# The sums made ahead get three buffers, a distance of ten weight tiles between load and use, and a place behind the newest low part on VectorE

## The chip, the cores and the metric

The kernel runs on one core of a Trainium2 chip. The metric is the device time of one execution in microseconds; the median of three runs of the kernel before is 1559.39 us (1559.27 to 1561.91).

## The reference

One decoder layer over 256 tokens of width 4096. One input projection feeds three token mixers and their gates; the branches are normalised, gated, joined and sent through one output projection.

```python
h = rmsnorm(x, ln_g)
proj = h @ w_in                                  # 4096 -> 12288
p_x, p_gate, q, k, v, a_gate, s_u, s_gate = jnp.split(proj, _SPLIT_OFFSETS, axis=-1)
y_pool = pool_mixer(p_x, w_pool, pool_scale)
y_attn = stick_breaking_attention(q, k, v)       # 16 heads of 128
y_ssm = s5_mixer(s_u, lam_re, ..., w_glu, b_glu) # diagonal state space, then h @ w_glu (1024 -> 2048)
y = concat(rmsnorm(y_*, g_*) * silu(gate_*))
return rmsnorm(x + y @ w_out) * final_g          # w_out 4096 -> 4096
```

## The kernel before

All large products are in float32, each made of three TensorE products of parts: the high part of the weights times the high part of the rows, low times high, and high times low. Weights come in **tiles** `w` of 128x1024 floats (512 KB): 384 for the input projection and 16 for the GLU, up to tile 400 (`OUT_FROM`), then 128 tiles for the output projection. For each tile ScalarE rounds the tile to its high part (`hi`, `hi_lo`, recorded at line 117) and VectorE subtracts it from the tile to give the low part (`lo`, line 105). TensorE then runs 12 matmuls of 128x512 on the tile (lines 308 to 310): `hi`, `lo`, `hi` for two row slots and two halves of the tokens. A tile has four buffers (`LOAD_AHEAD`), its parts have four (`RING`).

Beside the tiles run side chains: the state space scan (`ssm`, up to about tile 260: VectorE and ScalarE work, with small products `ps_bu` and `ps_y` on TensorE), attention (`ps_z`, `ps_av`), transposes (`ps_c`, `ps_t`), and gates. A tile scheduler puts VectorE, ScalarE and TensorE instructions into one fixed order for each engine, so an instruction whose data are late holds everything behind it on its engine. SyncE's DMA queue (SP) is in the order of the code; a DMA that has to wait for a buffer holds every later one.

The output projection uses a seven-product scheme for pairs of its 2x2 blocks, for which differences of four weight blocks are needed. For 34 of these blocks (`READY`, the words with "r" in `PLAN`) the differences are **made ahead**, by jobs of `sums_ahead` (line 179), one after another between tile 130 and tile 380. Each job loads two weight tiles of the output projection into `pre` (line 183, 2 x 512 KB), makes four subtractions of 128x512 in place on VectorE (shown as line 105), and stores the result to device memory as `sums` (line 197, 2 x 512 KB), from where the output stage loads it as `t`. The job is a generator with ten steps, pumped at 1.36 steps a tile: the two loads in steps one and two, the subtractions three to four steps later, the stores in two steps after those. `pre` has **one** buffer, so a job's first load waits for the stores of the job before. The loop over tiles issues, for tile i, first the load of tile i + 4 and the split of tile i + 2, then the products of tile i, then the side chains and the job's steps.

Of the kernel before, what the change touches and what calls it, by code (L numbers as in the profile page):

```python
# [12 lines left out]
F32 = mybir.dt.float32  # L13
# [4 lines left out]
ALU = mybir.AluOpType  # L18
PSUM = bass.MemoryType.PSUM

P = 128
# [3 lines left out]
NU = 512  # L25
# [20 lines left out]
READY = [(n, int(w[:-1])) for n, line in enumerate(PLAN) for w in line.split() if w[-1] == "r"]  # L46
ALL_SEVENS = sorted(set(sum(SEVENS, [])))
BACK = ((0, 768), (768, 768), (1536, 512))
READY_FROM = 130
READY_BY = 380  # L50
GATE_AT = (-1, 0, 6, 7)
WIDE = 2 * NU
WARM = 8
# [18 lines left out]
OUT_FROM = 24 * 16 + 4 * 4  # L72
# [3 lines left out]
def body(tc, a, out, ctx):  # L76
    nc = tc.nc
    V, S, T, G = nc.vector, nc.scalar, nc.tensor, nc.gpsimd
# [11 lines left out]
    def pool(name, bufs=1, **kw):  # L90
        return ctx.enter_context(tc.tile_pool(name=name, bufs=bufs, **kw))
# [5 lines left out]
    dp = pool("kept", space=bass.MemoryType.DRAM)  # L97
# [6 lines left out]
    def tt(o, x, y, op):  # L104
        V.tensor_tensor(o, x, y, op)  # L105
# [10 lines left out]
    def act(o, x, f, **kw):  # L116
        return S.activation(o, x, f, **kw)  # L117
# [34 lines left out]
    wtiles, htiles, ttiles, sums_kept = {}, {}, {}, {}  # L152
# [23 lines left out]
                nc.sync.dma_start(t[j], sums_kept[units[ui][1], s][:, j])  # L176
            ttiles[i] = t

    def sums_ahead(pl, job):
        b = pl.tile([P, 2, 2, NU], F32, tag="pre", bufs=1, name="pre")  # L180
        i = OUT_FROM + 32 * job[0] + 2 * ORDER[job[0]].index(job[1])
        for j in range(2):
            nc.sync.dma_start(b[:, j], a["ws"][i + j])
            yield
        yield
        yield
        x, y = b[:, 0], b[:, 1]
        tt(x[:, 0], y[:, 0], x[:, 0], ALU.subtract)
        tt(y[:, 0], y[:, 1], y[:, 0], ALU.subtract)
        yield  # L190
        tt(y[:, 1], y[:, 1], x[:, 0], ALU.subtract)
        tt(x[:, 1], x[:, 1], y[:, 1], ALU.subtract)
        yield
        yield
        kept_in = dp.tile([P, 2, 2, NU], F32, name="sums%d_%d" % job)
        for j in (1, 0):
            nc.sync.dma_start(kept_in[:, j], b[:, j])
            yield
        sums_kept[job] = kept_in
        yield  # L200

    def hi_lo(dst_hi, dst_lo, src):
        made = act(dst_hi, src, AF.Copy)
        tt(dst_lo, src, dst_hi.bitcast(F32), ALU.subtract)
        return made

    entries = [0]
# [105 lines left out]
    state = {"s7_out": {}, "out": False}  # L313
# [13 lines left out]
    def square_x(piece):  # L327
        xr = bp.tile([P, 2, NU], F32, tag="k4", bufs=K4, name="xsq")
        nc.sync.dma_start(xr, a["xr"][piece])
        square_sums(x_sums, xr, piece)  # L330

    def norm_x():
        s = cp.tile([P, 2], F32, name="s_x", tag="s_b", bufs=2)
        V.tensor_reduce(s, x_sums, mybir.AxisListType.X, ALU.add)
        rsqrt_mean(rtok, s, 2, D, cp, "rs")
# [409 lines left out]
    def scaled(ps, name):  # L745
        z = bp.tile([P, 2, NU], F32, tag="k4", bufs=K4, name=name)
        times_r(z, ps)
        return z
# [10 lines left out]
    def take_u(z, n):  # L759
        def gen():  # L760
            yield from channels(z, u_parts[n])
            u_done[0] = 4 * n + 4
        side_q.append(gen())
# [3 lines left out]
    def pump(q, n):  # L767
        while q and n > 0:
            try:
                if next(q[0], "end") == "end":  # L770
                    q.popleft()
                    continue
            except StopIteration:
                q.popleft()
                continue
            n -= 1
# [24 lines left out]
    rp = pre_ctx.enter_context(tc.tile_pool(name="ahead", bufs=1, side="right"))  # L801
# [8 lines left out]
    def constants():  # L810
        nc.sync.dma_start(ident, a["cst"][0])
        for i, dst in ((1, tneg), (2, oneneg), (3, maskb)):
            raw = mp.tile([P, P], F32, name="raw", tag="rb", bufs=1)
            nc.sync.dma_start(raw, a["cst"][i])
            act(dst, raw, AF.Copy)
        V.tensor_copy(identb, ident)
# [7 lines left out]
    def start_late():  # L824
        nonlocal lp
        drain(ssm_q)
        ssm_ctx.close()
        lp = late_ctx.enter_context(tc.tile_pool(name="late", bufs=1, side="right", reuse_waits="tile"))
# [10 lines left out]
    def start_out(n):  # L839
        if n == 0:  # L840
            start_end()
        c = [bank(n % 2 * 2 + t, "pm") for t in range(2)]
        o = ep.tile([P, 2, WIDE], F32, tag="o", bufs=2, name="o")
        for h in range(2):
            nc.sync.dma_start(o[:, :, h * NU:h * NU + NU], a["xr"][2 * n + h])
        return c, o
# [102 lines left out]
            hi_lo(hhl[:, 4 * n:4 * n + 4, 0, :], hhl[:, 4 * n:4 * n + 4, 1, :], u_parts[n])  # L949
        return hhl  # L950

    jobs = deque(READY)
    ready_q, ready_steps = deque(), [0]
    ready_q.extend(sums_ahead(rp, job) for job in jobs)
    ready_total = len(READY) * 10
    loaded = split_to = 0
    hhl = None
    delayed = []
    for i, (ui, at, h, s) in enumerate(subs):
        kind, c, nk = units[ui]  # L960
        if ui == 1 and s == 0:
            constants()
        if ui == 1 and s in SQUARE_AT:
            square_x(SQUARE_AT.index(s))
        if ui == 1 and s == 12:
            with tc.high_priority():
                norm_x()
                take_u(scaled(state.pop("ps0"), "suz"), 0)
        if at == 0 and h == 0:
            if ui == LATE_AT:  # L970
                start_late()
            if kind == "out":
                ps, state["o_n"] = start_out(c)
            else:
                ps = [pm.tile([P, NU], F32, tag="c%d" % t, bufs=2, name="pm") for t in range(2)]
            if kind == "glu" and hhl is None:
                hhl = split_glu()
        while loaded < min(len(subs), i + 1 + LOAD_AHEAD + (1 if state["out"] else 0)):
            if loaded == 0:
                load_first()  # L980
            else:
                if loaded < KT // 2:
                    load_x(loaded)
                load(loaded)
            loaded += 1
        while split_to < min(len(subs), i + 1 + SPLIT_AHEAD):
            split(split_to)
            split_to += 1
        if kind == "ag" and c == A_G + 1536 and s >= 2 and s % 2 == 0:
            take_back(s // 2 - 1)  # L990
        rows = hhl if kind == "glu" else xhl
        if seven(i):
            if h == 0:
                if s == SEVENS[c][0]:
                    drain(side_q)
                    pp = products(c)
                mm_seven(i, s, ps, pp, s == SEVENS[c][0], s == SEVENS[c][-1])
                j = SEVENS[c].index(s)
                if c == 3 and j < 2 * len(BACK):
                    lo, wide = BACK[j % len(BACK)]  # L1000
                    b = state["out_rows"].tile([P, 768], F32, tag="y7_%d" % s, name="back")
                    G.dma_start(b[:, 0:wide], state["done"][:, j // len(BACK), lo:lo + wide])
                    parts[j // len(BACK), lo] = b
                if s == SEVENS[c][-1]:
                    state["fg"] = load_fg(c)
                    state["joined"] = join_seven(pp, state["o_n"])
        else:
            pair = htiles.pop(i)
            late = i >= N_SUB - HELD
            into = [ps[t][h] for t in range(2)] if kind == "out" else ps  # L1010
            mm_tok(into, rows, (2 * s, 2 * s + 1), pair, at == 0, at == nk // 2 - 1, (0,) if late else (0, 1))
            if late:
                delayed.append((s, h, pair))
        if at == nk // 2 - 1 and h == (1 if kind == "out" else 0):
            n = nth.get(kind, 0)
            nth[kind] = n + 1
            if (kind, n) != ("out", 3):
                finish(kind, c, n, ps)
        if kind == "out" and c == 0 and h == 1 and s - 2 in ALL_SEVENS and s - 2 not in SEVENS[0]:
            rows_again(s - 2)  # L1020
        if i < OUT_FROM - 1:
            pump(side_q, 3)
        elif i - OUT_FROM in GATE_AT:
            pump(side_q, 1)
        want = (i - READY_FROM) * ready_total / (READY_BY - READY_FROM)
        while ready_steps[0] < want and ready_q:
            pump(ready_q, 1)
            ready_steps[0] += 1
        if i >= SSM_FROM:
            want = (i - SSM_FROM) * SSM_RATE  # L1030
            while ssm_steps[0] < want and ssm_q:
                pump(ssm_q, 1)
                ssm_steps[0] += 1

    last, fg = state["o_n"], state["fg"]
    sums = cp.tile([P, 2, 1], F32, name="last_sums")
# [120 lines left out]
```

## Time and profile before

| | |
|---|---|
| median of three runs | 1559.39 us |
| the profiled execution, its own time | 1561.89 us |
| its span, first to last instruction | 1560.1 us |
| TensorE matmuls busy | 1515.8 us of the span, 6842 matmuls |
| VectorE busy | 1219.6 us |
| ScalarE busy | 876.0 us |
| weight tiles loaded | 493 of 512 KB and 36 of 256 KB |
| `pre` loads, `sums` stores | 68 each, 512 KB each |
| moved by DMA | 424.50 MB, mean 272 GB/s |

The profiled execution lies at the upper end of the three runs, 2.5 us above their median. Times in rows count from the start of the span. "PE" is TensorE's matmuls, "DVE" VectorE, "ACT" ScalarE, "SPq" SyncE's DMA queue; "lo<-w,hi" is an instruction that reads tiles `w` and `hi` and writes `lo`. A number in brackets behind a row of the timeline is the time for which the engine stood idle before that row, and what released it.

### The profile page before, as it was taken

Reading aid. Unit: us, or ns where it says so; the run is one execution under the profiler, and the core shown is the slowest. Engines: PE = TensorE matmul, PEld = TensorE weight load, DVE = VectorE, ACT = ScalarE, POOL = GpSimd, SP = SyncE. Lnnn points to the kernel's source line nnn. Section 1 sums busy time; section 2 is a strip of 40 time slices with the busy share of each in tenths; the row PEclk is TensorE's granted clock in tenths of the full one; section 3 lists DMA queues with packets and bytes.
Section 4 is the critical chain, followed back from the end, with each engine's and each line's share of the span. In section 5 each row is a group of like instructions: output and inputs, shape, how many; then the busy total and the mean of one; then the engine's idle time right before and its main releaser. Section 6 shows DMA issues by size and latency. Waiting matters only on the chain.

```text
span 1560.1 us, 19835 instructions
## 1 busy us (share of the span) xinstructions
PE 1515.8 (97%) x6842; PEld 1233.4 (79%) x6842; DVE 1219.6 (78%) x1872; ACT 876.0 (56%) x1161; POOL 15.2 (1%) x31
## 2 busy tenths in 40 slices
PE   9999999999999989999999999998999999999996
PEld 7888788888787777778788888877778788888885
DVE  7479878898989887888775555665467998989896
ACT  7654546666554554445555543654446775757573
POOL 0000000000000000000000000000000000000000
PEclk9999999999999999999999999999999999999998
DMA  9866656666878767877688877697887899888894
GB/s 359 311 213 202 195 179 201 199 223 208 293 271 300 264 223 272 277 266 282 228 270 288 279 283 276 247 324 257 310 285 270 325 353 347 312 315 323 304 363 190
DMA packets 129508, 424.50 MB, mean 272 GB/s; under 512 B 15616, under 2 KB 21504, under 8 KB 129408
## 3 DMA queue, kind: packets, MB, share of 16 engines
q1 hardware_dynamic: 115504, 398.17, 72.4%
q10 hardware_dynamic: 10144, 10.92, 2.4%
q0 software_dynamic: 3760, 14.16, 2.3%
q8 instruction: 53, 0.87, 0.2%
q14 instruction: 47, 0.39, 0.1%
HBM read 371.28 MB, written 48.76 MB: 269 GB/s over the span
## 4 chain that ended last, share of the span: by engine, by line
PE 64%; DMA 16%; DVE 12%; issue 5%; ACT 2%; SPq 1%; ACTq 0%; DVEq 0%
PE pm L309 16%; PE pm L308 16%; PE pm L310 16%; PE p L276 7%; DMA pre<-in_ws 7%; PE pm L276 6%; DVE lo L105 4%; DMA sums<-pre 4%; DMA w<-in_ws 3%; DVE pre L105 2%; DVE ta L105 1%; DMA u<-uT 1%; ACT hi L117 1%; DVE et L114 1%; DVE tb L649 1%
## 5 line engine op out<-in xcount | busy, mean ns | idle before, releaser
L117 ACT ACTIVATE hi<-w 128x1024 fp32r<-128x1024 f32 (+1 forms) x531 | 536.6, 1018 | 444.9 <-PE pm L310 225.2
L105 DVE TENSOR_TENSOR lo<-w,hi 128x1024 fp32r<-128x1024 f32 (+1 forms) x531 | 617.0, 1171 | 160.2 <-ACT hi L117 158.6
L309 PE MATMUL pm<-lo,xhl 128*128 128x512 f32 x1712 | 672.5, 393 | 14.5 <-DVE lo L105 14.5
L310 PE MATMUL pm<-hi,xhl 128*128 128x512 f32 x1712 | 670.5, 392 | 0.0
L308 PE MATMUL pm<-hi,xhl 128*128 128x512 f32 x1712 | 660.5, 392 | 1.1 <-ACT xhl L117 0.6
L309 PEld LDWEIGHTS pm<-lo,xhl 128*128 128x128 f32 x1712 | 322.5, 188 | 88.7 <-DVE lo L105 20.8
L308 PEld LDWEIGHTS pm<-hi,xhl 128*128 128x128 f32 x1712 | 322.6, 189 | 71.0 <-issue 2.5
L310 PEld LDWEIGHTS pm<-hi,xhl 128*128 128x128 f32 x1712 | 322.7, 188 | 68.1 <-issue 2.3
L105 DVE TENSOR_TENSOR pre<-pre 128x512 f32<-128x512 f32 x136 | 93.4, 687 | 122.1 <-DMA pre<-in_ws 97.9
L117 ACT ACTIVATE hi<-t 128x1024 fp32r<-128x1024 f32 x84 | 87.0, 1053 | 40.1 <-DVE t L105 23.0
L105 DVE TENSOR_TENSOR lo<-t,hi 128x1024 fp32r<-128x1024 f32 x84 | 100.6, 1218 | 4.2 <-ACT hi L117 3.9
L276 PE MATMUL pm<-hi,xhl 128*128 128x512 f32 x168 | 66.0, 393 | 0.0
L276 PE MATMUL p<-hi,xhl 128*128 128x512 f32 x168 | 65.3, 391 | 0.0
L117 ACT ACTIVATE tr<-et,pw 128x32 f32<-128x32 f32 (+3 forms) x128 | 45.9, 387 | 33.6 <-DVE et L114 23.8
L276 PE MATMUL p<-hi,y 128*128 128x512 f32 x168 | 64.5, 392 | 0.0
L114 DVE SCALAR_TENSOR_TENSOR et<-et,pw,tr 128x16 f32<-128x16 f32 (+3 forms) x256 | 55.8, 274 | 3.1 <-ACT tr L117 2.8
L649 DVE TENSOR_TENSOR_SCAN tb<-rho,ta 128x256 f32<-128x256 f32 x64 | 40.6, 675 | 0.2
L276 PEld LDWEIGHTS pm<-hi,xhl 128*128 128x128 f32 x168 | 31.5, 188 | 7.4
L276 PEld LDWEIGHTS p<-hi,y 128*128 128x128 f32 x168 | 31.5, 187 | 7.3
L276 PEld LDWEIGHTS p<-hi,xhl 128*128 128x128 f32 x168 | 31.5, 187 | 7.2
L276 PE MATMUL pm<-hi,y 128*128 128x512 f32 x84 | 33.1, 394 | 0.0
L276 PE MATMUL p<-lo,y 128*128 128x512 f32 x84 | 33.0, 393 | 0.0
(245 smaller groups left out, 1128.7 us busy)
## 6 DMA issues: line engine op xcount, KB each, us to landing
w<-in_ws SPq DMA_DIRECT2D x493, 512.0 KB, 5.2
pre<-in_ws SPq DMA_DIRECT2D x68, 512.0 KB, 5.3
sums<-pre SPq DMA_DIRECT2D x68, 512.0 KB, 6.4
t<-sums SPq DMA_DIRECT2D x68, 512.0 KB, 6.9
w<-in_ws SPq DMA_DIRECT2D x36, 256.0 KB, 6.1
xsq<-in_xr SPq DMA_DIRECT2D x8, 512.0 KB, 7.0
o<-in_xr SPq DMA_DIRECT2D x8, 512.0 KB, 8.6
xt<-in_xT SPq DMA_DIRECT2D x15, 256.0 KB, 6.1
```

The costliest lines, as they stand in the source:

```text
L105: V.tensor_tensor(o, x, y, op)
L114: V.scalar_tensor_tensor(o, x, s, y, op0, op1)
L117: return S.activation(o, x, f, **kw)
L276: T.matmul(o, stat[:, p, :], pair[q][:, n], start=start and k == 0, stop=stop and k == 2, skip_group_check=True)
L308: T.matmul(ps[t], stat[:, slot, 0, sl], hi[:, n], start=begin, stop=False, skip_group_check=True)
L309: T.matmul(ps[t], stat[:, slot, 0, sl], lo[:, n], start=False, stop=False, skip_group_check=True)
L310: T.matmul(ps[t], stat[:, slot, 1, sl], hi[:, n], start=False, stop=end, skip_group_check=True)
L649: V.tensor_tensor_scan(tb[:, c, :], rho[:, pr:pr + 1].broadcast_to([P, L]), ta[:, c, :], 0.0, ALU.mult, ALU.add)
```

## The change

The generator becomes a table of steps. Job n begins at tile `126 + int(7.2 n)`. Its loads are issued at steps 0 and 1 of 15, its first two subtractions at step 10, the other two at step 11, its stores at steps 13 and 14, one step a tile. `pre` has three buffers. The first subtraction of each pair carries an order (no semaphore: both are on VectorE) behind the low part that was split last when the step is emitted; `hi_lo` keeps its name in `state["split"]`. The number of jobs, loads, subtractions and stores stays.

```diff
-READY_FROM = 130
-READY_BY = 380
+READY_FROM = 126
+READY_EVERY = 7.2
+READY_GAP = 10
+READY_BUFS = 3
...
-    def sums_ahead(pl, job):
-        b = pl.tile([P, 2, 2, NU], F32, tag="pre", bufs=1, name="pre")
+    def after_split(op):
+        tc.add_manual_dep(
+            op.ins, state["split"],
+            mybir.DependencyInfo(mybir.DependencyClass.NoSync, mybir.DependencyReason.DATA),
+            reason="not before its data are there",
+        )
+
+    def sums_ahead(n, job, step):
         i = OUT_FROM + 32 * job[0] + 2 * ORDER[job[0]].index(job[1])
-        for j in range(2):
-            nc.sync.dma_start(b[:, j], a["ws"][i + j])
-            yield
-        yield
-        yield
+        if step == 0:
+            ahead[n] = rp.tile([P, 2, 2, NU], F32, tag="pre", bufs=READY_BUFS, name="pre")
+        if step < 2:
+            nc.sync.dma_start(ahead[n][:, step], a["ws"][i + step])
+            return
+        b = ahead[n]
         x, y = b[:, 0], b[:, 1]
-        tt(x[:, 0], y[:, 0], x[:, 0], ALU.subtract)
-        tt(y[:, 0], y[:, 1], y[:, 0], ALU.subtract)
-        yield
-        tt(y[:, 1], y[:, 1], x[:, 0], ALU.subtract)
-        tt(x[:, 1], x[:, 1], y[:, 1], ALU.subtract)
...
+        if step == READY_GAP:
+            after_split(V.tensor_tensor(x[:, 0], y[:, 0], x[:, 0], ALU.subtract))
+            tt(y[:, 0], y[:, 1], y[:, 0], ALU.subtract)
+        elif step == READY_GAP + 1:
+            after_split(V.tensor_tensor(y[:, 1], y[:, 1], x[:, 0], ALU.subtract))
+            tt(x[:, 1], x[:, 1], y[:, 1], ALU.subtract)
+        elif step == READY_GAP + 3:
+            sums_kept[job] = dp.tile([P, 2, 2, NU], F32, name="sums%d_%d" % job)
+        if step in (READY_GAP + 3, READY_GAP + 4):
+            j = READY_GAP + 4 - step
+            nc.sync.dma_start(sums_kept[job][:, j], b[:, j])
 
     def hi_lo(dst_hi, dst_lo, src):
         made = act(dst_hi, src, AF.Copy)
-        tt(dst_lo, src, dst_hi.bitcast(F32), ALU.subtract)
+        state["split"] = V.tensor_tensor(dst_lo, src, dst_hi.bitcast(F32), ALU.subtract).ins.name
...
+    ahead, steps = {}, {}
+    for n, job in enumerate(READY):
+        for step in range(READY_GAP + 5):
+            steps.setdefault(READY_FROM + int(n * READY_EVERY) + step, []).append((n, job, step))
...
-        want = (i - READY_FROM) * ready_total / (READY_BY - READY_FROM)
-        while ready_steps[0] < want and ready_q:
-            pump(ready_q, 1)
-            ready_steps[0] += 1
+        for step in steps.get(i, ()):
+            sums_ahead(*step)
```

What moves is first shown on SyncE's queue, at the job for output block (3, 10), about 1090 to 1100 us into the span before the change. `w_` and a number are the loads of weight tiles, `pre_9372` and `pre_9518` the loads and stores of two jobs that follow each other in the one buffer.

```order
L197 DMA sums3_9_9479<-pre_9372 128x1024
L172 DMA w_9481<-in_ws 128x1024
L197 DMA sums3_9_9479<-pre_9372 128x1024
L172 DMA w_9500<-in_ws 128x1024
L183 DMA pre_9518<-in_ws 128x1024
L172 DMA w_9520<-in_ws 128x1024
L183 DMA pre_9518<-in_ws 128x1024
L172 DMA w_9539<-in_ws 128x1024
```

The same place of the queue after the change; line numbers are those of the changed code (207 the stores, 193 the loads of `pre`, 174 the loads of `w`).

```order
L207 DMA sums3_9_9464<-pre_9170 128x1024
L174 DMA w_9466<-in_ws 128x1024
L207 DMA sums3_9_9464<-pre_9170 128x1024
L193 DMA pre_9485<-in_ws 128x1024
L174 DMA w_9487<-in_ws 128x1024
L193 DMA pre_9485<-in_ws 128x1024
L174 DMA w_9506<-in_ws 128x1024
L174 DMA w_9524<-in_ws 128x1024
```

Loads of `pre` still follow stores closely, but the buffer that is loaded (`pre_9485`) is another than the one just stored (`pre_9170`); the job after this one (`pre_9621`) takes up the buffer of `pre_9170` again.

On VectorE, before: the four subtractions of `pre_9518` among the low parts of the tiles.

```order
L105 TENSOR_TENSOR lo_9503<-w_9461,hi_9502 128x1024
L105 TENSOR_TENSOR lo_9523<-w_9481,hi_9522 128x1024
L105 TENSOR_TENSOR pre_9518<-pre_9518 128x512 x2
L105 TENSOR_TENSOR lo_9542<-w_9500,hi_9541 128x1024
L105 TENSOR_TENSOR pre_9518<-pre_9518 128x512 x2
L105 TENSOR_TENSOR lo_9560<-w_9520,hi_9559 128x1024
```

On VectorE, after: those of `pre_9485`, whose loads stand around `w_9487` in the queue above.

```order
L211 TENSOR_TENSOR lo_9645<-w_9602,hi_9644 128x1024
L211 TENSOR_TENSOR lo_9663<-w_9623,hi_9662 128x1024
L198 TENSOR_TENSOR pre_9485<-pre_9485 128x512
L107 TENSOR_TENSOR pre_9485<-pre_9485 128x512
L211 TENSOR_TENSOR lo_9683<-w_9642,hi_9682 128x1024
L201 TENSOR_TENSOR pre_9485<-pre_9485 128x512
L107 TENSOR_TENSOR pre_9485<-pre_9485 128x512
L211 TENSOR_TENSOR lo_9727<-w_9660,hi_9726 128x1024
```

Before, the first subtraction stands ahead of the low part of `w_9500`, a tile that is loaded before `pre_9518` is. After, it stands behind the low part of `w_9623`, the eighth tile loaded after the first half of `pre_9485`. In all 34 jobs the distance so counted is one to three tiles ahead of the loads before the change, and seven tiles behind the second load after it.

More of the change, by code (lines that the diff above doesn't have):

```diff
@@ L177, in load @@
             ttiles[i] = t
-    def sums_ahead(pl, job):
-        b = pl.tile([P, 2, 2, NU], F32, tag="pre", bufs=1, name="pre")
-        i = OUT_FROM + 32 * job[0] + 2 * ORDER[job[0]].index(job[1])
-        for j in range(2):
-            nc.sync.dma_start(b[:, j], a["ws"][i + j])
-            yield
-        yield
-        yield
-        x, y = b[:, 0], b[:, 1]
-        tt(x[:, 0], y[:, 0], x[:, 0], ALU.subtract)
-        tt(y[:, 0], y[:, 1], y[:, 0], ALU.subtract)
-        yield
-        tt(y[:, 1], y[:, 1], x[:, 0], ALU.subtract)
-        tt(x[:, 1], x[:, 1], y[:, 1], ALU.subtract)
[L193 to L200, printed above, removed]
+    def after_split(op):
[5 more added lines that the diff above has]
+    def sums_ahead(n, job, step):
+        i = OUT_FROM + 32 * job[0] + 2 * ORDER[job[0]].index(job[1])
+        if step == 0:
[4 more added lines that the diff above has]
+        b = ahead[n]
+        x, y = b[:, 0], b[:, 1]
+        if step == READY_GAP:
[9 more added lines that the diff above has]
+            nc.sync.dma_start(sums_kept[job][:, j], b[:, j])
     def hi_lo(dst_hi, dst_lo, src):
         made = act(dst_hi, src, AF.Copy)
-        tt(dst_lo, src, dst_hi.bitcast(F32), ALU.subtract)
+        state["split"] = V.tensor_tensor(dst_lo, src, dst_hi.bitcast(F32), ALU.subtract).ins.name
         return made
@@ L950, in split_glu @@
         return hhl
[L952 to L955, printed above, removed]
+    ahead, steps = {}, {}
+    for n, job in enumerate(READY):
+        for step in range(READY_GAP + 5):
+            steps.setdefault(READY_FROM + int(n * READY_EVERY) + step, []).append((n, job, step))
+    assert max(steps) < OUT_FROM
     loaded = split_to = 0
```

## The prediction

> **What bounds the kernel now.** I read the page's head first, then the windows by stage, then who waited for whom, then the timeline at one wait. The page's first lines:
>
> ```profile
> span 1560.1 us, 19835 instructions
> PE 1515.8 (97%) x6842; PEld 1233.4 (79%) x6842; DVE 1219.6 (78%) x1872; ACT 876.0 (56%) x1161; POOL 15.2 (1%) x31
> ```
>
> TensorE is the bound: its matmuls cover 1515.8 of 1560.1 us, and the change takes no matmul away. So all that can be won is time in which TensorE stands, or runs slowly. The windows by stage (columns: TensorE busy, weight loads, VectorE, ScalarE, GpSimd, granted clock, DMA share, GB/s) say where that is:
>
> ```profile
> 385.00:480.00 95.00, 95.00 (x429) 76.98 (x428) 86.66 (x149) 49.01 (x68) 0.54 (x1) 1.00 0.83 289
> 480.00:800.00 320.00, 304.84 (x1419) 244.64 (x1418) 268.91 (x467) 161.38 (x229) 1.07 (x2) 0.99 0.76 261
> 800.00:960.00 160.00, 160.00 (x737) 133.24 (x737) 90.91 (x93) 76.34 (x85) 0.53 (x1) 1.00 0.80 281
> 960.00:1160.00 200.00, 187.28 (x842) 152.73 (x841) 121.22 (x139) 103.72 (x129) 5.39 (x10) 0.98 0.79 280
> ```
>
> TensorE stands 320 - 304.84 = 15.2 us in the first marked stretch (480 to 800) and 200 - 187.28 = 12.7 us in the second (960 to 1160), 27.9 together, and not at all in the other two. The jobs of sums made ahead run over just this time, from 385.6 to about 1160:
>
> ```profile
> L183 SPq DMA_DIRECT2D pre<-in_ws x68: 327/402/1241, 385.6 to 1145.7; - x68
> DMA to landing us min/median/max: 3.1/5.3/8.4
> L105 DVE TENSOR_TENSOR pre<-pre 128x512 f32<-128x512 f32 x136 | 93.4, 687 | 122.1 <-DMA pre<-in_ws 97.9
> SPq L183 <- DMA sums<-pre: 130.5, 35, 8.2
> ```
>
> VectorE does 93.4 us of work in the 136 subtractions and stands 122.1 us ahead of them, mostly for the load of `pre`. That load in turn was held on SyncE's queue for 130.5 us by the store of the job before, because there is one buffer. The timeline shows what TensorE has to do with it (the number in brackets is the idle time ahead of the row):
>
> ```profile
> 1098.49 1.23 DVE L105 TENSOR_TENSOR lo<-w,hi 128x1024 fp32r<-128x1024 f32 x1 [1.88 <-ACT hi L117]
> 1107.54 1.42 DVE L105 TENSOR_TENSOR pre<-pre 128x512 f32<-128x512 f32 x2 [7.83 <-DMA pre<-in_ws]
> 1108.88 1.22 DVE L105 TENSOR_TENSOR lo<-w,hi 128x1024 fp32r<-128x1024 f32 x1
> ```
>
> The low part at 1108.88 is held behind a subtraction that waits 7.83 us; TensorE, which in 1100 to 1110 is busy for only 6.81 us (row below), needs that low part. I looked at each of the 20 waits of TensorE in the two marked stretches in this way: all but one have such a subtraction, idle for 0.9 to 8.1 us, in the 14 us ahead of them. The exception is the first GLU product at 999 us, where VectorE splits the rows.
>
> **A second loss is the clock.** In four windows of 10 us the granted clock falls, each time behind such a wait; two windows with as large a wait keep it:
>
> ```profile
> 600.00:610.00 10.00, 7.90 (x32) 5.94 (x33) 9.88 (x15) 4.94 (x8) 0.53 (x1) 0.83 0.53 172
> 760.00:770.00 10.00, 7.93 (x28) 6.12 (x27) 7.26 (x11) 2.85 (x3) 0.00 (x0) 0.83 0.39 142
> 1060.00:1070.00 10.00, 9.76 (x41) 8.35 (x42) 7.30 (x9) 4.32 (x7) 1.08 (x2) 0.84 0.75 258
> 1100.00:1110.00 10.00, 6.81 (x31) 5.29 (x29) 2.42 (x3) 2.07 (x2) 1.08 (x2) 1.00 0.95 351
> 1110.00:1120.00 10.00, 9.85 (x36) 8.04 (x37) 7.24 (x8) 4.24 (x4) 0.00 (x0) 0.83 0.75 252
> 1150.00:1160.00 10.00, 7.15 (x32) 5.60 (x31) 6.68 (x8) 3.15 (x4) 0.00 (x0) 1.00 0.85 309
> 550.00:560.00 10.00, 7.42 (x34) 5.86 (x33) 10.00 (x15) 4.41 (x6) 0.00 (x0) 1.00 0.51 181
> ```
>
> Each dip costs 10 x (1 - 0.83) = 1.7 us (1.6 for the one at 0.84): 3.4 in the first stretch, 3.3 in the second, 6.7 in all, counted as busy time in the windows.
>
> **A third piece is hidden by the way ends are drawn.** Two matmuls in a row, and one behind a wait:
>
> ```profile
> 555.63 0.39 PE L309 MATMUL pm<-lo,xhl 128*128 128x512 f32 x1
> 555.86 0.39 PE L310 MATMUL pm<-hi,xhl 128*128 128x512 f32 x1
> 558.82 0.50 PE L704 MATMUL ps_z<-ah,tneg 128*128 128x512 f32 x1 [2.58 <-ACT ah L117]
> ```
>
> They start 0.23 us apart but last 0.39, so each wait is shown 0.16 us too short. With the waits counted below, 12 and 8, that is 1.9 and 1.3 us. What the waits cost in all: first stretch 15.2 + 3.4 + 1.9 = 20.5, second 12.7 + 3.3 + 1.3 = 17.3, together **37.8 us**.
>
> **The change, part by part.** The sum is made against the profiled execution's own 1561.89 us.
>
> *Three buffers.* No instruction is added. A job's first load no longer waits for the last store of the job before; it takes over a buffer whose store was issued seven tiles earlier. A tile is 12 matmuls x 0.23 = 2.8 us, so that is 20 us against stores that land in 6.4 us at the median (last row below); the 130.5 us of SyncE's queue go to nothing. What is late next there is the wait of a `w` load for its own buffer (first row below, 684.8 us), which is the normal state: the queue is ahead.
>
> ```profile
> SPq L172 <- DVE lo L105: 684.8, 310, 12.6
> SPq L197 <- DVE pre L105: 8.8, 10, 1.5
> sums<-pre SPq DMA_DIRECT2D x68, 512.0 KB, 6.4
> ```
>
> *Ten tiles between load and use.* The first subtraction stands nine tiles behind the second load, 9 x 2.8 = 25 us against a longest landing of 8.4. VectorE's 122.1 us ahead of the subtractions go too. What holds a low part next is VectorE's own work. In the first stretch that is 268.9 us against 304.8 us of TensorE work, 88%, so it fits; from 385 to 480 it was 86.7 of 95 (91%), with the jobs running, and TensorE stood 0.00 us. In the second stretch it is 121.2 of 187.3. The queue that the loads are moved past is SyncE's alone (GpSimd's and ScalarE's DMAs stay); bytes stay too, 0.76 of the DMA engines over 320 us becomes about 0.81 over 300, and 385 to 480 ran at 0.83 without a wait.
>
> *Behind the newest low part.* Both are on VectorE, so no semaphore is added, only a place. Four subtractions of 0.69 us a job now stand behind two low parts instead of partly ahead of them. Their price lies between a gain of 0.69 for each that no longer stands ahead of a low part that TensorE waits for, and a loss of the same for the side chains behind them. I take zero: nobody waits for the subtractions themselves, and the count stays at 93.4 us.
>
> *Stores behind the subtractions.* A store now stands one to two tiles behind its subtraction. In 63 of 68 cases the subtraction is ahead of the low part for which the next `w` load waits anyway, so it adds nothing; in five it is one to four VectorE instructions behind, at most 4 x 0.69 = 2.8 us. Price between 0 and 5 x 2.8 = 14 us of queue time. I take 0, by the second row above: ten such waits took 8.8 us before, none over 1.5, and loads run four tiles (11 us) ahead.
>
> *Start and pace.* From tile 126 and one job in 7.2 tiles instead of 7.35: 2% more of 2.75 us a job, nothing.
>
> **What stays.** TensorE's waits in the two stretches, by whom it waited for:
>
> ```profile
> PE pm L309 <- DVE lo L105: 5.4, 5, 2.1
> PE ps_z L704 <- ACT ah L117: 3.3, 2, 2.6
> PE ps_y L661 <- DVE ao L719: 2.6, 1, 2.6
> PE ps_c L755 <- DVE tb L105: 1.5, 2, 1.1
> PE ps_y L661 <- DVE s L105: 1.2, 1, 1.2
> PE ps_y L661 <- DVE tb L105: 1.0, 1, 1.0
> ...
> PE pm L309 <- DVE lo L105: 8.4, 5, 3.3
> PE ps_t L359 <- DVE gl L114: 3.5, 2, 2.9
> PE pm L308 <- DVE gl L105: 0.7, 1, 0.7
> ```
>
> The first six are the first stretch, the last three the second. In the second stretch VectorE has time to spare, and I let all go but the last row, 0.7 + 0.2 = 0.9: 17.3 - 0.9 = 16.4 won. In the first, the waits for low parts go, but `ps_z`, `ps_y` and `ps_c` (3.3 + 2.6 + 1.5 + 1.2 + 1.0 = 9.6 us, seven waits) are side products that stand in TensorE's order three to four tiles ahead of where VectorE must then be, with VectorE at 88%. There I keep half: 4.8 + 7 x 0.16 / 2 = 5.4. So 20.5 - 5.4 = 15.1 won. Sum: 16.4 + 15.1 = 31.5, and 1561.9 - 31.5 = **1530.4**. The profiled execution lies 2.5 us above the median of the runs before. I take nothing off for that: what differs between runs of one program is likely just these waits, and their floor is shared. It is in the low end instead.
>
> **Rivals.**
>
> *Every wait goes.* For it: no subtraction can wait any more. Against it: the tight side products. 1561.9 - 37.8 = 1524.1, and 2.5 less if the profiled run's surplus is something else: 1521.6.
>
> *The clock dips stay.* They do not follow waits strictly: 1150:1160 and 550:560 stand 2.9 and 2.6 us without a dip, 760:770 stands 2.1 with one. Were they set by something else, 6.7 us stay: 1530.4 + 6.7 = 1537.1. [...] The trace speaks against it, since all four dips stand right behind a wait of 2 us or more.
>
> *The side products keep all their waits, and VectorE's load is the cause in the first stretch.* Then only the second stretch is won: 1561.9 - 16.4 = 1545.5. Against it: each wait there has an idle VectorE ahead of it.
>
> *Slower.* The pairs of subtractions stand firmly between low parts, ahead of the chains that feed `ps_y` and `ps_z`, and TensorE, in order, waits there once a job. A wait like the longest for `ps_y`, with its dip, costs 2.6 + 1.7 + 0.2 = 4.5. Up to 800 us there are (800 - 385.6) / (774 / 34) = 18 jobs: 18 x 4.5 = 81 in place of 20.5, so 1561.9 - 16.4 - 20.5 + 81 = 1606. It turns slower than before from (16.4 + 20.5) / 4.5 = 8 of the 18 jobs. Against it: two subtractions are 1.4 us, and the parts' ring is four tiles, 11 us.
>
> *The change doesn't do what it says.* Only if data landed later than 25 us after the load, or another wait took TensorE's place one for one: 1562. Landings of 8.4 us at most speak against it.
>
> **How the numbers follow.** Forecast 1530.4: 0.52. Every wait goes: 0.16. Dips stay: 0.10. Side products keep theirs: 0.14. No change: 0.03. Slower: 0.05. The range reaches from 1521.6 to the third rival, 1546 rounded; some of that case lies above it, with the last two. A measurement of this kernel tells about 0.2%, 3 us, from no change. Faster 0.92, same 0.03, slower 0.05.
>
> **What would show it.** Right: the row of `pre` subtractions has next to no idle time for its load; SyncE's wait for `sums` is gone; 960 to 1160 (shifted) has TensorE busy all but a microsecond or two; fewer than two clock dips before the end. If `ps_z`, `ps_y` and `ps_c` still show 5 us or so, the half that I kept was right. Wrong: a wait for low parts that remains with VectorE busy throughout (load, not order), `w` loads late behind stores that wait for subtractions, or dips with no wait ahead of them.

## The result, and the profile after

The changed kernel takes 1523.61 us (median of four runs, 1522.72 to 1524.01) against 1559.33 us for the kernel before, run beside it; the ratio is 0.9769, with a 95% interval of 0.9752 to 0.9786. The forecast was 1530.4 with a range of 1521.6 to 1546, so the time lies in the range, 6.8 us below the forecast and on the rival "every wait goes" (1524.1). The profiled execution took 1522.72 us.

The page's head after:

```profile
span 1520.9 us, 19799 instructions
...
PE 1503.7 (99%) x6842; PEld 1230.8 (81%) x6842; DVE 1223.6 (80%) x1872; ACT 878.3 (58%) x1161; POOL 15.2 (1%) x31
...
PE 95%; DVE 2%; DMA 1%; issue 1%; ACT 1%; SPq 0%; DVEq 0%; ACTq 0%
```

The last line is the page's chain of work that ended last, by engine. 95% of it is TensorE's own work. In the page of before that line read as follows, so 16% and 12% of the chain had run through transfers and VectorE:

```profile
PE 64%; DMA 16%; DVE 12%; issue 5%; ACT 2%; SPq 1%; ACTq 0%; DVEq 0%
```

The windows of the same stages after the change (they begin and end earlier, since the time before them shrank):

```profile
360.00:460.00 100.00, 100.00 (x452) 81.16 (x451) 91.18 (x163) 57.54 (x83) 0.53 (x1) 1.00 0.81 284
460.00:770.00 310.00, 310.00 (x1466) 254.28 (x1465) 280.24 (x482) 168.67 (x236) 1.07 (x2) 1.00 0.81 283
770.00:930.00 160.00, 160.00 (x744) 132.45 (x743) 96.36 (x102) 77.19 (x88) 0.53 (x1) 1.00 0.81 284
930.00:1125.00 195.00, 194.27 (x897) 161.09 (x896) 128.26 (x143) 109.17 (x133) 5.40 (x10) 1.00 0.83 300
```

TensorE (the second number) stands 0.7 us in all four together, where it stood 27.9, and the granted clock (1.00) does not dip. All of TensorE's waits that the trace names after the change:

```profile
PE ps_i L136 <- DVE zeros L133: 1.2, 1, 1.2
PE pm L315 <- DVE gl L107: 0.7, 1, 0.7
PE pm L315 <- ACT xhl L119: 0.7, 1, 0.7
PE pm L316 <- DVE lo L211: 0.7, 1, 0.7
PE pm L315 <- ACT hi L119: 0.5, 1, 0.5
```

The second is the GLU's first product, the one wait of the second stretch that the prediction kept. Those for `ps_z`, `ps_y` and `ps_c` are gone. Where the time was won shows when the same matmul is looked up in both profiles. Of the matmuls that write `pm`, number 2000 starts 490 us into the span in both. Number 3200 (815.5 us before) starts 21.6 us earlier after the change, number 3800 (961.1) still 21.6, number 4600 (1173.7) 39.0, and number 5600 39.3. So the first stretch gave 21.6 us, the second 17.4, and the rest next to nothing.

VectorE has no row any more that waits for `pre`; what is left on SyncE's queue, and what ScalarE waits for, is this:

```profile
SPq L174 <- DVE lo L211: 744.8, 364, 11.9
...
SPq L207 <- DVE pre L201: 20.4, 26, 4.3
...
SPq L207 <- DVE pre L107: 10.0, 13, 1.9
...
ACT hi L119 <- PE pm L317: 369.3, 272, 2.9
ACT hi L119 <- DMA w<-in_ws: 56.2, 56, 3.8
```

ScalarE's two rows before the change:

```profile
ACT hi L117 <- PE pm L310: 230.1, 176, 2.9
...
ACT hi L117 <- DMA w<-in_ws: 156.8, 106, 5.3
```

ScalarE now waits mostly for TensorE to give back a buffer of the parts (369.3 us, 230.1 before), which means that the splits more often run as far ahead as their four buffers let them; its waits for weight tiles fell from 156.8 us to 56.2. The stores wait longer for the subtractions than before (20.4 + 10.0 us in the two rows above, against 8.8), as they were built to, and TensorE has no wait that goes with it.

### The profile page after: what moved, and what is told of

It reads as the page before. It is cut to its first block, busy times and chain, and to the rows that moved or that the text cites. A ratio compares the mean times of both kernels' runs of the same rounds, so it can differ in the third digit from the quotient of the medians.

```text
span 1520.9 us, 19799 instructions
## 1 busy us (share of the span) xinstructions
PE 1503.7 (99%) x6842; PEld 1230.8 (81%) x6842; DVE 1223.6 (80%) x1872; ACT 878.3 (58%) x1161; POOL 15.2 (1%) x31
## 4 chain that ended last, share of the span: by engine, by line
PE 95%; DVE 2%; DMA 1%; issue 1%; ACT 1%; SPq 0%; DVEq 0%; ACTq 0%
PE pm L315 26%; PE pm L316 26%; PE pm L317 26%; PE p L283 8%; PE pm L283 6%; DMA w<-in_ws 1%; PE ps_y L668 1%; DVE lo L211 1%; PE ps_c L762 1%; PE ps_bu L641 1%; PE ps_p L450 0%; PE ps_t L366 0%; PE ps_z L693 0%; DVE ts L107 0%; PE ps_z L711 0%
## 5 line engine op out<-in xcount | busy, mean ns | idle before, releaser
L211 DVE TENSOR_TENSOR lo<-w,hi 128x1024 fp32r<-128x1024 f32 (+1 forms) x531 | 620.0, 1173 | 232.4 <-ACT hi L119 230.1
L107 DVE TENSOR_TENSOR pre<-pre 128x512 f32<-128x512 f32 x68 | 46.7, 687 | 0.9
```

Of the source, the lines that this page charges most:

```text
L211: state["split"] = V.tensor_tensor(dst_lo, src, dst_hi.bitcast(F32), ALU.subtract).ins.name
```

## The experiments

The change has three parts: buffers, a table of steps with a distance of ten tiles, and an order. The order of the instructions shows a fact that upsets the prediction's bookkeeping: **without the order, the table of steps hardly moves the subtractions.** In the changed kernel without its order (run e3 below) VectorE has the four subtractions of `pre_9485` here:

```
L211 TENSOR_TENSOR lo_9509<-w_9466,hi_9508 128x1024
L107 TENSOR_TENSOR pre_9485<-pre_9485 128x512 x4
L211 TENSOR_TENSOR lo_9527<-w_9487,hi_9526 128x1024
```

They stand behind the low part of `w_9466`, the tile requested just ahead of the first half of `pre_9485`, so as close to the load as in the kernel before. Over the 34 jobs of e3 the first subtraction stands one to three tiles ahead of the loads (two in 19 jobs, one in 13), as it did before the change (two in 28). My reading is that the scheduler takes an instruction up as soon as it reckons that its data are there, wherever the code emits it; the runs show only where it put them. So **theory A** says that the place on VectorE, set by the order, is what counts (a standing VectorE holds the low parts, as it held the one at 1108.88 before the change for 7.83 us); **theory B** says that the one buffer and the held queue are what counts.

### One part at a time

**e1: the kernel before, three buffers.**

```diff
-        b = pl.tile([P, 2, 2, NU], F32, tag="pre", bufs=1, name="pre")
+        b = pl.tile([P, 2, 2, NU], F32, tag="pre", bufs=3, name="pre")
```

> The kernel before with three buffers for pre and nothing else. Theory A (distance: VectorE stands because a subtraction comes less than one landing behind its load, one to two tiles of 2.8 us against 5 to 7 us): SyncE's wait for the stores (130.5 us) goes, but VectorE keeps 50 to 100 of its 122 us ahead of the subtractions, and the time is 1538 to 1552. Theory B (queue: the one buffer makes the loads late, the rest follows): VectorE's wait falls under 20 us, and the time is 1524 to 1530.

Measured: 1532.76 us (1531.29 to 1540.21), ratio 0.9822 (0.9789 to 0.9855). VectorE's waits for `pre` and its stages:

```profile
DVE pre L105 <- DMA pre<-in_ws: 78.2, 30, 7.3
...
480.00:790.00 310.00, 306.78 (x1451) 249.03 (x1450) 270.56 (x466) 165.56 (x235) 1.07 (x2) 1.00 0.77 275
...
950.00:1140.00 190.00, 186.11 (x857) 153.15 (x856) 119.38 (x136) 104.48 (x130) 5.37 (x10) 1.00 0.84 301
```

Theory A had VectorE's wait right (78 us in its 50 to 100) and the time wrong (1538 to 1552); theory B had both wrong. With 78 of 122 us still there, TensorE stands only 3.2 + 3.9 us in the two stretches. These 78 us of a standing VectorE cost 9 of the 37 us, much less than their share of the 122.

**e3: the changed kernel without the order.**

```diff
-            after_split(V.tensor_tensor(x[:, 0], y[:, 0], x[:, 0], ALU.subtract))
+            tt(x[:, 0], y[:, 0], x[:, 0], ALU.subtract)
...
-            after_split(V.tensor_tensor(y[:, 1], y[:, 1], x[:, 0], ALU.subtract))
+            tt(y[:, 1], y[:, 1], x[:, 0], ALU.subtract)
```

> The changed kernel without the order behind the newest low part: loads, stores and buffers as changed, but the scheduler puts the subtractions one to three tiles ahead of where the loads stand, as before the change. Theory A: the order carries the distance, so VectorE stands 50 to 100 us ahead of the subtractions again and the time is 1538 to 1552, like the three buffers alone. Theory B (and the prediction's own price of zero for the order): 1523 to 1527.

Measured: 1532.9 us (1529.93 to 1536.5), ratio 0.9814 (0.9786 to 0.9843), the time of the three buffers alone. VectorE stands again:

```profile
DVE pre L107 <- DMA pre<-in_ws: 74.1, 28, 6.7
```

So the table of steps without its order adds nothing to the three buffers. Theory B, and with it the price of 0 for the order, was wrong: taken out, the order costs 9 us. Theory A had the wait right and overrated the time here too.

**e6: the kernel before, with the order alone** (`after_split` and `state["split"]` as in the change; one buffer, the old generator).

```diff
-        tt(x[:, 0], y[:, 0], x[:, 0], ALU.subtract)
+        after_split(V.tensor_tensor(x[:, 0], y[:, 0], x[:, 0], ALU.subtract))
...
-        tt(y[:, 1], y[:, 1], x[:, 0], ALU.subtract)
+        after_split(V.tensor_tensor(y[:, 1], y[:, 1], x[:, 0], ALU.subtract))
```

> The kernel before with one buffer and its old steps, and only the order behind the newest low part added; the first subtraction moves back by two to three tiles (6 to 8 us). Theory A' (a held queue and a standing VectorE hurt only together; the place by the order is enough): VectorE's wait falls from 122 to 20 to 50 us, SyncE's 130 us for the stores stay, 1526 to 1538. Theory B' (the one buffer is the cause whatever the order): 1545 to 1560.

Measured: 1524.13 us (1522.36 to 1526.79), ratio 0.9766 (0.9734 to 0.9798): **the whole gain from the order alone**, better than theory A' had it (1526 to 1538, with a wait of 20 to 50 us). VectorE has no row that waits for `pre`, while SyncE's queue is held more than before, by loads that wait for the stores of the job before (first row) and by stores that wait for the subtractions, which stand later now (the other two):

```profile
SPq L190 <- DMA sums<-pre: 92.3, 33, 5.9
SPq L204 <- DVE pre L198: 92.2, 29, 6.1
...
SPq L204 <- DVE pre L105: 36.0, 24, 3.1
```

That is 220 us of held queue against 139 in the kernel before, and no loss that shows: 1524.1 us against 1523.6 for the change.

**e2: the changed kernel with two buffers**, where a job's load again stands directly behind the store that it has to wait for.

```diff
-READY_BUFS = 3
+READY_BUFS = 2
```

> The changed kernel with two buffers, so that a job's load again waits on SyncE's queue for the store just ahead of it (5 us, 32 times, 100 to 160 us in all), while the subtractions stay nine tiles behind their loads. Theory A: VectorE never waits for pre, weight tiles are loaded four ahead (11 us), so 1523 to 1527. Theory B: the held queue makes weight tiles late, TensorE waits 10 us or more, 1535 to 1550.

Measured: 1526.18 us (1525.78 to 1526.57), ratio 0.977 (0.9747 to 0.9794). The time is theory A's. The wait is back:

```profile
SPq L193 <- DMA sums<-pre: 151.4, 37, 6.3
```

The median is 2.6 us above that of the change, but the two kernels have the same ratio to the kernel before that ran beside them (0.977), so 2.6 us is the most that this wait costs.

**What follows.** The four corners, in us:

| | one buffer | three buffers |
|---|---|---|
| no order | 1560.7 (before) | 1532.8 (e1), 1532.9 (e3, with steps) |
| order | 1524.1 (e6) | 1523.6 (the change) |

The queue alone does not explain the 37 us: held for 150 to 220 us, with VectorE never standing for `pre`, it costs 0 to 3 us in e2 and e6. A VectorE that stands for 74 to 78 us, with the queue free, costs 9. That the two together cost 37 has two explanations, which these four corners do not tell apart. Either they hurt together, for instance because a `w` load needs both a free place in the queue and a low part that is done (before the change `w` loads waited 684.8 us for low parts, and the queue was held 130.5 us ahead of `pre` loads). Or a standing VectorE is the whole cause, and only its longer waits reach TensorE; then the buffers help because loads that go out earlier make those waits shorter. The runs of the next part bear on it. ScalarE's waits for weight tiles do not settle it, since they do not follow the time: 156.8 us before, 135.5 in e1, 83.6 in e3, 115.8 in e2, 103.9 in e6.

### How much distance, how many buffers

**e4, e7, e8: two steps between load and subtraction instead of ten,** with three, one and two buffers.

```diff
-READY_GAP = 10
+READY_GAP = 2
...
-READY_BUFS = 3
+READY_BUFS = 1
```

The last two lines are e7's; e8 has 2 there, and e4 leaves it at 3.

> The changed kernel with the subtractions two steps behind the loads instead of ten, three buffers and the order kept: the first subtraction stands about one tile closer than the second load allows. Theory A: VectorE waits 1 to 4 us a job, 30 to 100 us in all, and the time is 1532 to 1548. Theory B: 1523 to 1528.

> The changed kernel with one buffer and the subtractions two steps behind the loads, so that the store waits on SyncE's queue are back (130 to 160 us) while order and table of steps stay; one tile less distance than the order alone gives. Theory A': VectorE waits 40 to 90 us since the loads are issued late, with the queue held too, and the time is 1532 to 1548. If the time is 1522 to 1527, neither buffers nor distance matter, only the order does. Theory B': 1545 to 1560.

> The changed kernel with two buffers and the subtractions two steps behind the loads: a buffer is free eight tiles before it is taken again, so no store is waited for. All theories: as with three buffers and two steps, 1521 to 1524; it tells whether the third buffer and the eight further steps are worth anything.

Measured: e4 1522.13 us (1521.55 to 1523.1), ratio 0.9745 (0.9717 to 0.9774); e7 1523.92 (1521.56 to 1525.79), 0.9763 (0.9731 to 0.9795); e8 1522.74 (1521.87 to 1523.4), 0.9756 (0.9726 to 0.9785). In all three the first subtraction stands only one tile later than in most jobs of the kernel before. VectorE's waits for `pre` in e4, and in e7 with SyncE's:

```profile
DVE pre L198 <- DMA pre<-in_ws: 3.7, 4, 1.4
```

```profile
DVE pre L198 <- DMA pre<-in_ws: 23.4, 14, 3.5
...
SPq L193 <- DMA sums<-pre: 98.1, 34, 6.2
```

So theory A's 30 to 100 us for e4, and its time, fall: behind the order, two steps do what ten do. The time lies below what either theory said. And e7 is the case in which, by its expectation, neither buffers nor distance matter but only the order: 1522 to 1527 was written, 1523.9 came. Both its waits were smaller than expected, though: 98.1 us on the queue instead of 130 to 160, and 23.4 on VectorE instead of 40 to 90. e8 came as written.

What sets these times apart can be read job by job from the traces. The second column is how long after the second load of a job went out VectorE was ready for its first subtraction (median of 34 jobs); the third, in how many jobs it then stood for more than 3 us; the fourth, how often SyncE's queue stood for more than 5 us ahead of a `pre` load or a store of `sums`.

| run | VectorE ready after, us | stood over 3 us | queue held over 5 us | time, us |
|---|---|---|---|---|
| before | 2.7 | 19 | 10 | 1560.7 |
| e1 | 5.5 | 9 | 0 | 1532.8 |
| e3 | 6.1 | 11 | 0 | 1532.9 |
| e7 | 6.2 | 2 | 3 | 1523.9 |
| e4 | 8.1 | 0 | 0 | 1522.1 |
| e8 | 8.1 | 0 | 0 | 1522.7 |
| e6 | 9.1 | 0 | 10 | 1524.1 |
| e2 | 28.5 | 0 | 13 | 1526.2 |
| the change | 30.6 | 0 | 0 | 1523.6 |

The time goes with the third column and not with the fourth. In e7 both happen, a held queue and 23.4 us of short waits on VectorE, and nothing is lost. This speaks for VectorE's longer waits as the cause, helped by buffers only in that the loads go out earlier; but no run has the waits of the kernel before with a free queue, so it is not shown.

**e11 and e12: the changed kernel and e8 side by side,** because a difference of 0.1% is in question.

> The changed kernel as it is, beside the next one on the same chip: 1523 to 1524.

> Two buffers and two steps again, to tell it from the changed kernel: if the third buffer and the longer way cost nothing, the same within 0.1%; if the 2.8 us that stores and sums stand later, or fuller DMA queues, cost something, 1 to 2 us less.

Measured: e11 1524.46 us (1523.37 to 1525.12), ratio 0.9768 (0.9739 to 0.9798); e12 1522.66 (1521.86 to 1524.13), 0.9758 (0.9728 to 0.9787). e11 lies half a microsecond above what was written; e12 lies 1.8 us below e11, as the second half of its expectation had it. Of the six runs of each, one of e12 lies above the lowest of e11, and the others all below. So two buffers and two steps look better by about 0.1%, with 8 KB less a partition; the ratio intervals overlap, so it is a tendency and no more. Whether fuller queues or later stores make the difference was not tried.

### How much room VectorE has

The prediction kept half of the waits for side products because VectorE was 88% busy. Three kernels give it more work. They add instructions whose results nobody needs.

**e5: four more instructions a job, in place** (the maximum of a part with itself).

```diff
             tt(y[:, 0], y[:, 1], y[:, 0], ALU.subtract)
+            for part in (x[:, 0], y[:, 0]):
+                tt(part, part, part, ALU.max)
...
             tt(x[:, 1], x[:, 1], y[:, 1], ALU.subtract)
+            for part in (y[:, 1], x[:, 1]):
+                tt(part, part, part, ALU.max)
```

> The changed kernel with four more VectorE instructions of 128x512 a job (each takes the maximum of a part with itself), behind the subtractions. 136 x 0.6 us = 82 us more VectorE work; in 460 to 770 some 15 jobs add 37 us to its 280 of 310 us, so it is over-full there. Theory L (the load of VectorE is what makes ps_z, ps_y and ps_c wait, as the prediction had it when it kept half of their waits): TensorE waits 15 to 25 us again, 1538 to 1550. Theory S (they waited only behind a VectorE that stood; tiles split four ahead cover 11 us of lateness): only the excess of some 7 us and a few waits, 1525 to 1535.

Measured: 1608.62 us (1608.01 to 1611.43), ratio 1.031 (1.0271 to 1.0349): 85 us more than the change, beyond both theories. The added instructions took 0.67 to 0.69 us each, where 0.6 was written. The kernel does not tell them apart, since it did something else as well. The stores come behind the added instructions, which have no order and slid back among the side chains; SyncE's queue was held for them up to 10.2 us at a time, ScalarE waited 225.7 us for weight tiles (56.2 after the change), and TensorE waited for the splits rather than for side products:

```profile
SPq L211 <- DVE pre L107: 209.5, 35, 10.2
...
ACT hi L119 <- DMA w<-in_ws: 225.7, 150, 9.0
...
PE pm L319 <- ACT hi L119: 27.2, 24, 3.3
PE pm L320 <- DVE lo L215: 23.0, 36, 1.8
...
PE ps_z L715 <- ACT ah L119: 0.9, 1, 0.9
```

So a held queue went with a loss of 0 to 3 us in e2 and e6, where its longest holds for `pre` and `sums` were 6.3 and 6.1 us, and with 85 us here, where they reached 10.2. VectorE never stands for `pre` here, and between 480 and 800 us it is no fuller than after the change (284.70 of 320 us against 280.24 of 310). But the queue is held 16 times for over 6 us, where the kernel before has two such holds, e6 three and e2 four. That the long holds are the cause of the 85 us is argued, since the added work changed the order on VectorE as well.

**e10 and e9: two and four more subtractions a job into a tile of their own,** on two buffers and two steps.

```diff
             tt(y[:, 0], y[:, 1], y[:, 0], ALU.subtract)
+            more = rp.tile([P, NU], F32, tag="more", bufs=1, name="more")
+            for _ in range(1):
+                tt(more, y[:, 1], x[:, 1], ALU.subtract)
...
             tt(x[:, 1], x[:, 1], y[:, 1], ALU.subtract)
+            more = rp.tile([P, NU], F32, tag="more", bufs=1, name="more")
+            for _ in range(1):
+                tt(more, y[:, 1], x[:, 0], ALU.subtract)
```

That is e10; e9 has `range(2)` twice.

> The same with two more subtractions a job: 41 us more VectorE work, about 96% of TensorE's time in the busiest 300 us. Theory L: 1530 or more, with waits at ps_z, ps_y and ps_c. Theory S: 1521 to 1526.

> The kernel with two buffers and two steps, with four more subtractions of 128x512 a job into a tile of their own that nobody reads, so that stores wait for them less than they did with the doubled work in place: 82 us more VectorE work, about 102% of TensorE's time in the busiest 300 us. Theory L (side products wait from VectorE's load): 1545 or more. Theory S (slack of four tiles; only what does not fit is lost): 1527 to 1538.

Measured: e10 1544.25 us (1543.12 to 1548.19), ratio 0.9893 (0.9849 to 0.9937); e9 1568.79 (1561.32 to 1570.83), 1.0045 (1.0024 to 1.0067). The times are those of theory L. But the added subtractions have no order either, and wait for loads as the subtractions of e3 did (rows of e10: VectorE, then TensorE):

```profile
DVE more L107 <- DMA pre<-in_ws: 42.3, 18, 8.0
...
PE ps_z L717 <- ACT ah L119: 6.3, 2, 6.0
PE pm L322 <- DVE lo L217: 4.4, 6, 1.1
PE pm L321 <- ACT hi L119: 3.7, 3, 2.2
PE ps_z L717 <- DVE ax L107: 2.3, 1, 2.3
```

So in e10 some 47 us of work (68 subtractions at the 0.687 us of those of `pre` before the change; the expectation had 41) came with 42 us of standing. Side products do wait again (8.6 us at `ps_z`); what pure load costs without standing stays open, and with it the choice between theories L and S.

## Why the prediction was right, and where it was off

- **Bound and place: right.** The time came out of the two stretches (21.6 + 17.4 us) and next to nowhere else. The ceiling of 37.8 us, made of TensorE's waits and dips, stands against 39.2 by the profiled executions (1561.89 - 1522.72); the rest may be waits too short to be shown, which no run tells.
- **Three buffers and the distance: the waits went as written** (SyncE's for `sums` ahead of a `pre` load, 130.5 us, and VectorE's ahead of the subtractions, 122.1 us, have no row any more). The 25 us written between load and use came out as 27 to 43 in the trace. But the prediction credited the distance to the table of steps, and gave the order **a price of zero**. That is the step that failed: the order carries the distance. Alone it brings all of the gain (e6), and without it 9 us are lost (e3). The ten tiles and the three buffers, which the sum leaned on, add nothing that shows once the order is there (e8, e7). That the sum was not hurt is luck: all parts were there together, so it did not matter which was credited.
- **Second stretch, 16.4 us: right.** It gave 17.4. The one wait that was kept, at the GLU, is the one that is there (0.7 us).
- **First stretch, 15.1 us with half of the side products' waits kept (5.4 us): mis-sized.** It gave 21.6, and the waits that were kept measured zero. This is most of the 6.8 us between forecast and result. With VectorE at 90% (280.24 of 310 us) side products do not wait at all, so a load of that size alone does not make them wait. In e10 some wait again, but there VectorE also stands for loads, so no run shows a load at which they would wait for load alone.
- **Clock dips: right that they go.** The rival in which they stay (1537.1) is out: the stages with jobs run at 1.00 after the change, in e1 and in e3, and e2, e4, e6, e7 and e8 have the mean clock of the change over the whole execution (0.996 or 0.997, against 0.993 before). None of these has a wait of TensorE over 2.2 us in the stages with jobs. e5, e9 and e10, whose longest waits are 3.3, 5.0 and 6.0 us, dip: the mean clock is 0.98 in 480 to 800 us of e5, 0.97 and 0.98 in 460 to 800 us of e9 and e10. How long a wait must be for a dip is not shown: before the change one of 2.1 us has a dip behind it and one of 2.9 us has none.
- **Stores behind the subtractions, 0 us: right in time, wrong in the count.** Stores waited 39 times and 30.4 us, where five times and at most 14 us were written, without a wait of TensorE that goes with it; in e2 even 151.4 us of another wait on that queue cost at most 2.6.
- **Slower, and no change: did not come.** While the jobs run, TensorE's only wait is the one at the GLU.

## What to carry to other kernels

Where a scheduler sets the order of an engine, look at the order it made before crediting a distance written in the code: here, instructions emitted ten tiles later stood in nearly the same place until an order pinned them. When an engine stands for a load and a queue stands for a store, try the cures one at a time before paying for both: here the buffers alone gave three quarters of the gain and the order alone all of it, and the order needs no buffer. A test that adds work must pin that work too, or it measures where the scheduler put it.

## What the runs showed that was not expected

- A `pre` load that no store holds back landed later. Its median from issue to landing went from 5.3 us before to 7.5 with three buffers alone (first row below) and 7.1 after (second row), while the weight tiles' stayed at 4.9 to 5.3. The other runs agree: 5.1 to 5.7 us where loads wait for stores (e2, e6, e7), 7.0 to 7.7 where they do not (e3, e4, e8). Why is not shown.

```profile
pre<-in_ws SPq DMA_DIRECT2D x68, 512.0 KB, 7.5
```

```profile
pre<-in_ws SPq DMA_DIRECT2D x68, 512.0 KB, 7.1
```

- A dip can last. In e10, behind the longest wait of all these runs (5.98 us at `ps_z`), the clock stays at half (0.52) through a whole window of 10 us, in which TensorE has short waits too:

```profile
750.00:760.00 10.00, 10.00 (x52) 8.41 (x52) 10.00 (x16) 4.48 (x7) 0.00 (x0) 1.00 0.84 274
760.00:770.00 10.00, 3.70 (x14) 2.52 (x12) 8.57 (x15) 4.36 (x5) 0.00 (x0) 0.80 0.66 252
770.00:780.00 10.00, 7.15 (x28) 6.37 (x29) 9.16 (x27) 5.92 (x13) 0.00 (x0) 0.52 0.17 52
780.00:790.00 10.00, 10.00 (x47) 8.30 (x47) 9.69 (x16) 6.32 (x7) 0.00 (x0) 1.00 0.13 34
```

Before the change, shorter waits of 2.1 to 3.3 us cost one dip of about 1.7 us or none. What makes a dip last is not shown.
